# A two-layer decoder trunk with experts: weights of the experts loaded in 2 MB pieces, and the optional slots served after every piece

## The chip, the cores and the metric

The kernel runs on one core of one Trainium2 chip. The metric is device time in microseconds (us) of one execution; the figure compared is the median of several executions. One core has the engines PE (matrix products, with its weight loads, PEld), DVE and ACT (element-wise work out of PSUM and SBUF), POOL, and SP, which here issues the loads; 16 DMA engines move the data.

## The reference

256 tokens of width 1024 in float32 go through two layers. Layer 0 is retention (4 heads) and a dense SwiGLU of width 2816; layer 1 is a sparse attention with three branches and a mixture of experts. Each half is followed by a layer norm of alpha times its input plus its output. The part that the change touches is the mixture of experts:

```python
logits = (xf @ w_router).astype(jnp.float32)
top_v, top_i = lax.top_k(logits, TOP_K)              # 2 of 8 experts for each token
w = jax.nn.softmax(top_v, axis=-1)
gate = jnp.sum(jax.nn.one_hot(top_i, N_EXPERTS, dtype=jnp.float32) * w[..., None], axis=1)
for e in range(N_EXPERTS):
    out = out + gate[:, e:e + 1] * swiglu(xf, w_in[e], w_out[e])   # w_in 1024 x 7168, w_out 3584 x 1024
```

512 token places fall on 8 experts, 64 for each in the mean. The weights of one expert are 44 MB, of all eight 352 MB, and each is read once.

## The kernel before

All weights come from HBM through one ordered list of loads (`order`). A load (class `Raw`) is a tile of 128 partitions by 2048 floats: 1 MB, 8 KB in a row for each partition, laid out on the host so that it is contiguous. Units are the parts of a load that a step reads; when the last unit of a load has been read, `release` (L198) frees its buffer and at that point of the program issues the next load of the list. SP issues every load in program order. There are three kinds of buffers: 8 tiles `raw`, 2 tiles `more`, which come when the attention's buffers are given back (`moe_open`, L1316), and 6 tiles `ext`, which come when the buffers of split weights are given back (`moe_more`, L1323). So up to 16 MB of expert weights stand in SBUF. Ahead of the experts' list 87 single loads are made: 32 for the retention, 33 for the dense SwiGLU, 22 for the attention.

The work is a list of steps in a fixed order. An expert has 96 token places (slots) in three groups of 32, g = 0, 1, 2. Its hidden width is cut into four parts s = 0 to 3. For each part, `w_in` (L1192) multiplies the gathered tokens with 8 loads (4 for s = 3) of the input weights, `w_out` (L1250) multiplies the result of the part before with 4 loads (2 for s = 3) of the output weights, and then `h_transpose` (L1231) turns the hidden values. So an expert takes 28 + 14 = 42 loads, all experts 336. The step list puts `w_out` of a part behind `w_in` of the next one: `w_out` of the last part of expert e comes behind `w_in` of the first part of expert e + 1. The transposes for the scatter, the scatter itself and the gather for a later pair of experts stand between these steps.

Groups 0 and 1 are always computed, by `first` (L1206, L1264), load by load. Group 2 (slots 65 to 96) is needed only where more than 64 tokens chose the expert. Its count is in a register of PE; `rest` (L1214, L1274) holds a branch on it. It stands once in each `w_in` and each `w_out`, behind all loads of that step: where the count is over 64, PE reads all these loads again for group 2; where it isn't, `w_in` (and `w_out` of part 0) zeroes the PSUM bank of group 2 in the other arm. Both `first` and `rest` hold a unit of every load, so none of the loads of a step is released before its `rest`.

```python
            for i, u in enumerate(us):
                step([u[0]], first(i, u[0]), look=0)
            step([u[1] for u in us], rest, look=0)
```

The program is one instruction stream for each engine with semaphores between them.

Of the kernel before, what the change touches and what calls it, by code (L numbers as in the profile page):

```python
# [29 lines left out]
NE = 8  # L30
# [1 line left out]
NEG = -1e30  # L32

NRAW = 8
NMORE = 2
NEXT = 6
NHL = 6
LOOK = 3

# [36 lines left out]
class Raw:  # L76
    def __init__(self, parts):
        self.parts = parts
        self.kind = None
        self.last = False  # L80
        self.ap = None
        self.left = 0


class Unit:
# [10 lines left out]
def tile_decoder(ctx, tc, x, ret_w_in, ret_gn_g, ret_w_out, nsa_w_kv, cmp_k_pe, cmp_k_w1, cmp_k_w2,  # L96
# [76 lines left out]
    def raw(*parts):  # L173
        r = Raw(parts)
        raws.append(r)
        return r

    state = {"loaded": 0, "conv": 0, "raw": [], "more": [], "ext": []}

    def load(r):  # L180
        if r.kind == "more":
            r.ap = ptile([128, 2048], F32, "more", bufs=NMORE, lv=0)
        elif r.kind == "ext":
            r.ap = side["pool"].tile([128, 2048], F32, name="ext", tag="ext", bufs=NEXT)
        else:
            r.ap = sb.tile([128, 2048], F32, name="raw", tag="raw", bufs=NRAW)
        for view, src in r.parts:
            nc.sync.dma_start(view(r.ap), src)

    def load_next(kind="raw"):  # L190
        i = state["loaded"]
        if i < len(order) and not (kind != "raw" and order[i].last):
            state["loaded"] += 1
            order[i].kind = kind
            state[kind].append(order[i])
            load(order[i])

    def release(r):  # L198
        r.left -= 1
        held = state[r.kind]  # L200
        while held and held[0].left == 0:
            held.pop(0)
            load_next(r.kind)

    def convert(u, hi=None, lo=None):
        if not u.conv or u.hi is not None:
# [92 lines left out]
    def whole(n):  # L299
        return lambda a: a[:, :n]  # L300
# [75 lines left out]
    def ptile(shape, dt, tag, bufs=1, lv=-1):  # L376
        return phases[lv][1].tile(shape, dt, name=tag, tag=tag, bufs=bufs)
# [656 lines left out]
    if stop not in ("r1", "r2", "r3"):  # L1034
# [141 lines left out]
                                           skip_runtime_bounds_check_because="each of the S tokens counts at most once")  # L1176
            return f

        def units_m(block):

            r = raw((whole(2048), block))
            return [Unit(r, lambda a: a, conv=False) for _ in range(2)]

        def ws(s):
            return 256 if s < 3 else 128
# [6 lines left out]
        def w_in(e, s, us):  # L1192

            n, kl = 2 * ws(s), 8 // len(us)

            def mm(i, u, gs):
                v = u.view(u.raw.ap).rearrange("p (k j n) -> p k j n", k=kl, j=4)
                for g in gs:
                    for kk in range(kl):
                        k = i * kl + kk  # L1200
                        for j in range(4):
                            nc.tensor.matmul(M["A", g][j * 32:(j + 1) * 32, :n],  # L1202
                                             M["xg", e // 2][:, k, e % 2, g * 32:(g + 1) * 32], v[:, kk, j],
                                             start=k == 0, stop=k == KD - 1, skip_group_check=True)

            def first(i, u):  # L1206
                def f():
                    if i == 0:
                        for g in range(NG):
                            M["A", g] = bank("mm")  # L1210
                    mm(i, u, (0, 1))
                return f

            def rest():  # L1214
                with tc.If(M["n", e] > 64) as cmp:
                    for i, u in enumerate(us):
                        mm(i, u[1], (2,))
                with cmp.Else():
                    zero(M["A", 2])
                w = ws(s)  # L1220
                sh = ptile([128, NG, 256], F32, "msh")
                for g in range(NG):
                    nc.scalar.activation(sh[:, g, :w], M["A", g][:, :w], AF.Silu)  # L1223
                    nc.vector.tensor_mul(sh[:, g, :w], sh[:, g, :w], M["A", g][:, w:2 * w])  # L1224
                M["h"] = sh

            for i, u in enumerate(us):
                step([u[0]], first(i, u[0]), look=0)
            step([u[1] for u in us], rest, look=0)

        def h_transpose(s):  # L1231
            def f():
# [17 lines left out]
        def w_out(e, s, us):  # L1250

            hT = {}

            def mm(i, u, gs):
                v = u.view(u.raw.ap).rearrange("p (c h n) -> p c h n", c=2, h=2)
                for g in gs:
                    for c in range(2):
                        j, cc = (i, c) if s < 3 else (2 * i + c, 0)
                        for h in range(2):
                            q = (2 * h + c) * 32  # L1260
                            nc.tensor.matmul(M["y", g][q:q + 32], hT[0][:, g, cc, j * 32:(j + 1) * 32], v[:, c, h],  # L1261
                                             start=s == 0 and i == 0, stop=s == 3 and i == 1, skip_group_check=True)

            def first(i, u):  # L1264
                def f():
                    if i == 0:
                        hT[0] = M["hT"]
                        if s == 0:
                            for g in range(NG):
                                M["y", g] = bank("acc")  # L1270
                    mm(i, u, (0, 1))
                return f

            def rest():  # L1274
                with tc.If(M["n", e] > 64) as cmp:
                    for i, u in enumerate(us):
                        mm(i, u[1], (2,))
                if s == 0:
                    with cmp.Else():
                        zero(M["y", 2])  # L1280
                if s == 3:
                    y = ptile([128, 2, NG, 512], F32R, "yhl")
                    for g in range(NG):
                        if e < NE - 1:
                            split(y[:, 0, g], y[:, 1, g], M["y", g])
                        else:
                            nc.scalar.activation(y[:, 0, g], M["y", g], AF.Copy, scale=M["gs"][:, g:g + 1])  # L1287
                            nc.vector.scalar_tensor_tensor(y[:, 1, g], M["y", g], M["gs"][:, g:g + 1],  # L1288
                                                           y[:, 0, g].bitcast(F32), op0=ALU.mult, op1=ALU.subtract)
                    M["yhl"] = y  # L1290

            for i, u in enumerate(us):
                step([u[0]], first(i, u[0]), look=0)
            step([u[1] for u in us], rest, look=0)

        def scatter_mm(e, t, ps, start):

# [76 lines left out]
        for e in range(NE):  # L1374
            step([], count(e), look=0)
            for s in range(4):
                nl, nb = (8, 4) if s < 3 else (4, 2)
                w_in(e, s, [units_m(wst['moe_a'][28 * e + 8 * s + i]) for i in range(nl)])
                if prev:
                    w_out(*prev)  # L1380
                step([], h_transpose(s), look=0)
                if s == 0:
                    step([], transpose_S(e) if e == 0 else scatter(e - 1), look=0)
                    if e == 0:
                        step([], moe_gates, look=0)
                if s == 1 and e:
                    step([], transpose_S(e), look=0)
                if s == 2 and e % 2 and e < NE - 1:
                    step([], lambda j=e // 2 + 1: build_S(j), look=0)
                    for kq in range(4):  # L1390
                        step([], gather(e // 2 + 1, kq), look=0)
                if s == 2 and e == NE - 1:
                    step([], slot_gates, look=0)
                prev = e, s, [units_m(wst['moe_o'][14 * e + 4 * s + i]) for i in range(nb)]
        step([], sum_open, look=0)
        w_out(*prev)
        gbr = raw(*[(lambda a, i=i: a[:, i * D:(i + 1) * D],
# [82 lines left out]
    flat = [u for us, _, _ in steps for u in us]  # L1480
    order = []
    for u in flat:
        if u.raw not in order:
            order.append(u.raw)
    for _ in range(2):
        load_next()
    pos = 0
# [54 lines left out]
    yield w[:, 6].reshape(2, 2, 128, 1024).transpose(0, 2, 1, 3).reshape(2, 128, 2048)  # L1542


def _laid_out(v):
    ri, q, mi, mo = v['ret_w_in'][0], v['nsa_w_q'][0], v['moe_w_in'][0], v['moe_w_out'][0]
    return {
        'ret_b': _cols_b(ri[:, :2048]), 'ret_a': _cols_a(ri[:, 2048:]), 'ret_o': _rows(v['ret_w_out'][0]),
        'ffn_b': _cols_b(v['ffn_w_in'][0]), 'ffn_o': _rows(v['ffn_w_out'][0]),
        'kv_a': _cols_a(v['nsa_w_kv']), 'k_w1': _rows(v['cmp_k_w1']), 'v_w1': _rows(v['cmp_v_w1']),  # L1550
        'q0': _cols_a(np.concatenate([q[:, :256], q[:, 1024:]], 1), 304), 'q1': _cols_a(q[:, 256:1024], 256),
        'nsa_o': _rows(v['nsa_w_out'][0]),
        'moe_a': np.concatenate([b for e in range(NE) for b in _expert_in(mi[e])]),
        'moe_o': np.concatenate([b for e in range(NE) for b in _expert_out(mo[e])]),
    }


# [31 lines left out]
```

## Time and profile before

| | us |
|---|---|
| median of 3 runs | 1461.58 |
| runs | 1460.39 to 1463.45 |
| the profiled execution | 1460.46 |
| its span, first to last instruction | 1458.7 |
| PE busy | 1355.4 (93%) |
| PE weight loads busy | 755.2 (52%) |
| DVE busy | 471.3 (32%) |
| ACT busy | 347.0 (24%) |
| POOL busy | 62.7 (4%) |
| HBM read | 447.74 MB, 308 GB/s over the span |

The layers before the experts take about 588 us, the experts the rest. Busy time of PE is modelled to the end of each product, and products overlap; so the time of a load's products is taken from start to start. A product of float32 shows as two records: 16 records of `128x512` are the 8 products of one load for groups 0 and 1, 8 records are the 4 products of one load for group 2.

### The profile page before, as it was taken

Reading aid. Unit: us, or ns where it says so; the run is one execution under the profiler, and the core shown is the slowest. Engines: PE = TensorE matmul, PEld = TensorE weight load, DVE = VectorE, ACT = ScalarE, POOL = GpSimd, SP = SyncE. Lnnn points to the kernel's source line nnn. Section 1 sums busy time; section 2 is a strip of 40 time slices with the busy share of each in tenths; the row PEclk is TensorE's granted clock in tenths of the full one; section 3 lists DMA queues with packets and bytes.
Section 4 is the critical chain, followed back from the end, with each engine's and each line's share of the span. In section 5 each row is a group of like instructions: output and inputs, shape, how many; then the busy total and the mean of one; then the engine's idle time right before and its main releaser. Section 6 shows DMA issues by size and latency. Waiting matters only on the chain. (4 is left out here: it accounts for less than half of the span.)

```text
span 1458.7 us, 25366 instructions
## 1 busy us (share of the span) xinstructions
PE 1355.4 (93%) x11073; PEld 755.2 (52%) x11073; DVE 471.3 (32%) x845; ACT 347.0 (24%) x653; POOL 62.7 (4%) x74
## 2 busy tenths in 40 slices
PE   8999999999999988998999988888999988889995
PEld 7888888999978657432334332232333342222341
DVE  5755875554674886100100201001101101001002
ACT  4433434434534562200101110011001010000002
POOL 3101101000011000100000000000000000000000
PEclk9999999999999898999999999999999999999997
DMA  9736444544615308599999999999999999999970
GB/s 388 271 139 220 158 168 176 201 180 173 250 59 209 124 1 319 209 418 419 419 419 418 412 418 419 419 418 419 419 416 416 419 419 419 419 418 419 418 306 32
DMA packets 64022, 450.78 MB, mean 309 GB/s; under 512 B 7233, under 2 KB 7393, under 8 KB 10641
## 3 DMA queue, kind: packets, MB, share of 16 engines
q1 hardware_dynamic: 62208, 443.77, 75.4%
q0 software_dynamic: 1536, 4.98, 1.0%
q8 instruction: 106, 1.74, 0.5%
q14 instruction: 28, 0.22, 0.0%
q10 hardware_dynamic: 144, 0.07, 0.0%
HBM read 447.74 MB, written 1.05 MB: 308 GB/s over the span
## 5 line engine op out<-in xcount | busy, mean ns | idle before, releaser
L1202 PE MATMUL mm<-raw,xg 128*32 128x512 f32 (+1 forms) x2416 | 242.9, 544 | 11.5 <-DMA raw<-w_moe_a_dram 11.4
L1224 DVE TENSOR_TENSOR msh<-msh,mm 128x256 f32<-128x256 f32 (+1 forms) x96 | 35.5, 387 | 509.3 <-ACT msh L1223 509.3
L215 DVE TENSOR_TENSOR wlo<-raw,whi 128x1024 fp32r<-128x1024 f32 (+2 forms) x162 | 187.6, 1208 | 32.1 <-ACT whi L214 31.8
L1202 PE MATMUL mm<-ext,xg 128*32 128x512 f32 (+1 forms) x1808 | 178.8, 538 | 14.5 <-DMA ext<-w_moe_a_dram 14.5
L1202 PEld LDWEIGHTS mm<-raw,xg 128*32 128x32 f32 x2416 | 74.5, 110 | 164.4 <-issue 119.1
L214 ACT CAST whi<-raw 128x1024 fp32r<-128x1024 f32 (+2 forms) x162 | 153.7, 1008 | 18.6 <-PE acc L224 12.2
L1223 ACT ACTIVATE msh<-mm 128x256 f32<-128x256 f32 (+1 forms) x96 | 32.4, 357 | 492.9 <-PE mm L1202 492.9
L348 PE MATMUL mm<-xTh,whi 128*128 128x256 f32 x448 | 126.5, 282 | 1.6 <-ACT whi L214 1.6
L350 PE MATMUL mm<-xTh,wlo 128*128 128x256 f32 x448 | 125.9, 281 | 0.5 <-DVE wlo L215 0.5
L1261 PE MATMUL acc<-raw,hT 128*32 128x512 f32 x1000 | 116.5, 594 | 10.4 <-DMA raw<-w_moe_o_dram 9.2
L349 PE MATMUL mm<-xTl,whi 128*128 128x256 f32 x448 | 125.7, 281 | 0.0
L1202 PEld LDWEIGHTS mm<-ext,xg 128*32 128x32 f32 x1808 | 55.2, 110 | 129.3 <-issue 77.8
L1261 PE MATMUL acc<-ext,hT 128*32 128x512 f32 x864 | 98.4, 594 | 8.7 <-DMA ext<-w_moe_o_dram 8.7
L348 PEld LDWEIGHTS mm<-xTh,whi 128*128 128x128 f32 x448 | 84.7, 189 | 3.1 <-ACT whi L214 2.0
L350 PEld LDWEIGHTS mm<-xTh,wlo 128*128 128x128 f32 x448 | 84.7, 189 | 0.8 <-DVE wlo L215 0.8
L349 PEld LDWEIGHTS mm<-xTl,whi 128*128 128x128 f32 x448 | 84.7, 189 | 0.8
L1246 DVE COPY hT<-mm 128x256 f32<-128x256 f32 (+1 forms) x32 | 12.4, 389 | 223.2 <-PE mm L1239 223.2
L1261 PEld LDWEIGHTS acc<-raw,hT 128*32 128x32 f32 x1000 | 31.9, 110 | 87.9 <-issue 61.5
L1244 ACT COPY hT<-acc 128x512 f32<-128x512 f32 (+1 forms) x32 | 17.1, 536 | 230.6 <-PE acc L1239 150.1
L1202 PE MATMUL mm<-more,xg 128*32 128x512 f32 (+1 forms) x640 | 65.1, 535 | 4.9 <-DMA more<-w_moe_a_dram 4.8
L1261 PEld LDWEIGHTS acc<-ext,hT 128*32 128x32 f32 x864 | 26.4, 110 | 76.1 <-issue 50.8
L222 PE MATMUL mm<-whi,xTh 128*128 128x512 f32 (+1 forms) x144 | 55.6, 386 | 0.2 <-ACT xTh L227 0.2
(325 smaller groups left out, 1676.4 us busy)
## 6 DMA issues: line engine op xcount, KB each, us to landing
raw<-w_moe_a_dram SPq DMA_DIRECT2D x113, 1024.0 KB, 19.9
ext<-w_moe_a_dram SPq DMA_DIRECT2D x82, 1024.0 KB, 19.9
raw<-w_moe_o_dram SPq DMA_DIRECT2D x55, 1024.0 KB, 19.9
ext<-w_moe_o_dram SPq DMA_DIRECT2D x44, 1024.0 KB, 19.9
more<-w_moe_a_dram SPq DMA_DIRECT2D x29, 1024.0 KB, 19.9
raw<-w_ffn_b_dram SPq DMA_DIRECT2D x22, 1024.0 KB, 5.0
raw<-w_ret_a_dram SPq DMA_DIRECT2D x16, 1024.0 KB, 8.9
more<-w_moe_o_dram SPq DMA_DIRECT2D x13, 1024.0 KB, 19.9
```

Of the source, the lines that this page charges most:

```text
L214: nc.scalar.copy(u.hi, v)
L215: nc.vector.tensor_sub(u.lo, v, u.hi.bitcast(F32))
L222: nc.tensor.matmul(ps, xh, wh, start=start, stop=False, skip_group_check=True)
L348: nc.tensor.matmul(ps, u.hi[:, k], xh[:, k], start=start and k == 0, stop=False, skip_group_check=True)
L349: nc.tensor.matmul(ps, u.hi[:, k], xl[:, k], start=False, stop=False, skip_group_check=True)
L350: nc.tensor.matmul(ps, u.lo[:, k], xh[:, k], start=False, stop=k == KD - 1, skip_group_check=True)
L1202: nc.tensor.matmul(M["A", g][j * 32:(j + 1) * 32, :n], M["xg", e // 2][:, k, e % 2, g * 32:(g + 1) * 32], v[:, kk, j], start=k == 0, stop= ...
L1223: nc.scalar.activation(sh[:, g, :w], M["A", g][:, :w], AF.Silu)
L1224: nc.vector.tensor_mul(sh[:, g, :w], sh[:, g, :w], M["A", g][:, w:2 * w])
L1244: nc.scalar.copy(dst, src)
L1246: nc.vector.tensor_copy(dst, src)
L1261: nc.tensor.matmul(M["y", g][q:q + 32], hT[0][:, g, cc, j * 32:(j + 1) * 32], v[:, c, h], start=s == 0 and i == 0, stop=s == 3 and i == 1, ...
```

## The change

Two neighbouring loads of one expert step become one of 2 MB (class `Slot`, with `wide` as its source). The host lays the two blocks out side by side (`_pairs`), so that each partition has 16 KB in a row. The 8 `raw` tiles become one tile `ring` of 8 places; a single load takes one place, a pair two neighbouring ones, and a pair that would begin at an odd place leaves one place empty until that pair is released. `more` is one tile of 2 MB, `ext` are three. A pair is released when both of its halves have been read. `rest` is called behind every second load, for these two alone; the zeroing arm and the element-wise work stay with the last call (the zeroing of `w_out` with its first).

```diff
-NMORE = 2
-NEXT = 6
+NMORE = 1
+NEXT = 3
...
+    ring = sb.tile([128, NRAW * 2048], F32, name="ring")
+    state = {"at": 0, "free": NRAW, "loaded": 0, "conv": 0, "raw": [], "more": [], "ext": []}
+
+    def load(z):
+        n = len(z.raws)
+        if z.kind == "more":
+            ap = ptile([128, n * 2048], F32, "more", bufs=NMORE, lv=0)
+        elif z.kind == "ext":
+            ap = side["pool"].tile([128, n * 2048], F32, name="ext", tag="ext", bufs=NEXT)
         else:
-            r.ap = sb.tile([128, 2048], F32, name="raw", tag="raw", bufs=NRAW)
-        for view, src in r.parts:
-            nc.sync.dma_start(view(r.ap), src)
+            i = (state["at"] + z.room - n) % NRAW
+            state["at"] += z.room
+            ap = ring[:, i * 2048:(i + n) * 2048]
+        if z.wide is not None:
+            nc.sync.dma_start(ap, z.wide() if callable(z.wide) else z.wide)
...
+            if kind == "raw":
+                n = len(order[i].raws)
+                order[i].room = n + state["at"] % n
+                if state["free"] < order[i].room:
+                    return False
+                state["free"] -= order[i].room
...
     def release(r):
         r.left -= 1
-        held = state[r.kind]
-        while held and held[0].left == 0:
-            held.pop(0)
-            load_next(r.kind)
+        kind = r.slot.kind
+        held = state[kind]
+        while held and all(q.left == 0 for q in held[0].raws):
+            z = held.pop(0)
+            if kind != "raw":
+                load_next(kind)
+            else:
+                state["free"] += z.room
+                while load_next():
+                    pass
...
-            def rest():
+            def rest(i):
                 with tc.If(M["n", e] > 64) as cmp:
-                    for i, u in enumerate(us):
-                        mm(i, u[1], (2,))
+                    for j in (i, i + 1):
+                        mm(j, us[j][1], (2,))
+                if i + 2 < len(us):
+                    return
                 with cmp.Else():
                     zero(M["A", 2])
...
             for i, u in enumerate(us):
                 step([u[0]], first(i, u[0]), look=0)
-            step([u[1] for u in us], rest, look=0)
+                if i % 2:
+                    step([v[1] for v in us[i - 1:i + 1]], lambda i=i: rest(i - 1), look=0)
...
+def _pairs(blocks):
+
+    b = np.concatenate(list(blocks))
+    return b.reshape(-1, 2, 128, 2048).transpose(0, 2, 1, 3).reshape(-1, 128, 4096)
```

## Rows read from the trace of the kernel before

**Rows 1.** The page's 40 slices: busy tenths of DMA, then GB/s.
```profile
DMA  9736444544615308599999999999999999999970
GB/s 388 271 139 220 158 168 176 201 180 173 250 59 209 124 1 319 209 418 419 419 419 418 412 418 419 419 418 419 419 416 416 419 419 419 419 418 419 418 306 32
```
**Rows 2.** Busy time by stretch: PE, PEld, DVE, ACT, POOL; PEclk, DMA share, GB/s.
```profile
590.00:600.00 10.00, 10.00 (x96) 2.99 (x92) 0.00 (x0) 0.33 (x1) 0.00 (x0) 1.00 0.01 2
...
646.00:1310.00 664.00, 606.58 (x5871) 211.72 (x5871) 68.66 (x155) 59.40 (x143) 5.94 (x12) 1.00 1.01 418
740.00:840.00 100.00, 98.25 (x1000) 37.73 (x993) 11.80 (x27) 9.88 (x23) 1.02 (x2) 1.00 1.01 416
...
1326.00:1438.00 112.00, 111.23 (x1093) 40.53 (x1087) 12.58 (x26) 10.37 (x24) 0.00 (x0) 1.00 0.79 323
```
**Rows 3.** Timeline of PE, head of expert 7: start, us, operation, count [idle <-releaser].
```profile
1305.27 1.92 PE L1261 MATMUL acc<-raw,hT 128*32 128x512 f32 x16 [0.58 <-DMA raw<-w_moe_o_dram]
1307.37 0.41 PE L1239 MATMUL acc<-ident,msh 128*128 128x128 f32 x2 [0.18 <-PEq L1275]
...
1307.97 1.92 PE L1202 MATMUL mm<-raw,xg 128*32 128x512 f32 x16
1310.24 1.93 PE L1202 MATMUL mm<-raw,xg 128*32 128x512 f32 x16 [0.35 <-DMA raw<-w_moe_a_dram]
...
1325.19 1.92 PE L1202 MATMUL mm<-ext,xg 128*32 128x512 f32 x16 [0.57 <-DMA ext<-w_moe_a_dram]
1326.93 2.76 PE L1202 MATMUL mm<-raw,xg 128*32 128x512 f32 x24
...
1332.08 1.90 PE L1202 MATMUL mm<-ext,xg 128*32 128x512 f32 x16
1333.80 3.62 PE L1261 MATMUL acc<-ext,hT 128*32 128x512 f32 x32
```
**Rows 4.** Timeline of SP: the loads issued from 468 to 607 us.
```profile
468.89 84.29 SPq L188 DMA_DIRECT2D raw<-w_moe_a_dram  x7
553.29 0.85 SPq L188 DMA_DIRECT2D more<-w_moe_a_dram  x2
560.45 0.33 SPq L188 DMA_DIRECT2D raw<-w_moe_a_dram  x1
569.23 3.50 SPq L188 DMA_DIRECT2D ext<-w_moe_a_dram  x6
602.61 1.97 SPq L188 DMA_DIRECT2D raw<-w_moe_o_dram  x4
```
**Rows 5.** Timeline of PE, head of expert 0.
```profile
588.45 12.22 PE L1202 MATMUL mm<-raw,xg 128*32 128x512 f32 x112
600.49 1.90 PE L1202 MATMUL mm<-more,xg 128*32 128x512 f32 x16
602.20 0.40 PE L1189 MATMUL mm<-zb 128*32 128x512 bf16 x4
```
**Rows 6.** DMA from 646 to 1310 us: packets, MB; then the loads' own queue.
```profile
DMA packets 38040, 277.53 MB, mean 418 GB/s; under 512 B 4223, under 2 KB 4223, under 8 KB 4223
...
q1 hardware_dynamic: 37976, 276.52, 100.6%
```
**Rows 7.** DMA from 700 to 1300 us by queue: packets, MB, share of 16 engines.
```profile
q1 hardware_dynamic: 34309, 249.82, 100.6%
q8 instruction: 54, 0.88, 0.6%
```
**Rows 8.** DMA from 450.5 to 455 us, mostly rows of 4 KB.
```profile
DMA packets 448, 1.80 MB, mean 400 GB/s; under 512 B 49, under 2 KB 49, under 8 KB 408
...
q1 hardware_dynamic: 448, 1.80, 99.0%
```
**Rows 9.** Branches of `w_in` (L1215) and `w_out` (L1275): ns min/median/max.
```profile
L1215 PEldq COMPARE_BRANCH  x44: 65/179/860, 599.6 to 1416.8; - x44
L1275 PEldq COMPARE_BRANCH  x44: 65/178/357, 623.0 to 1435.0; - x44
```

More of the change, by code (lines that the diff above doesn't have):

```diff
@@ L78, in __init__ @@
         self.parts = parts
-        self.kind = None
+        self.slot = None
         self.last = False
@@ L82, in __init__ @@
         self.left = 0
+class Slot:
+    def __init__(self, raws, wide=None):
+        self.raws = raws
+        self.wide = wide
+        self.last = raws[0].last
+        self.kind = None
+        self.room = 0
+        for r in raws:
+            r.slot = self
 class Unit:
@@ L176, in raw @@
         return r
[L178 to L184, printed above, removed]
-        else:
-            r.ap = sb.tile([128, 2048], F32, name="raw", tag="raw", bufs=NRAW)
-        for view, src in r.parts:
-            nc.sync.dma_start(view(r.ap), src)
+    ring = sb.tile([128, NRAW * 2048], F32, name="ring")
[6 more added lines that the diff above has]
+            ap = side["pool"].tile([128, n * 2048], F32, name="ext", tag="ext", bufs=NEXT)
+        else:
+            i = (state["at"] + z.room - n) % NRAW
[3 more added lines that the diff above has]
+            nc.sync.dma_start(ap, z.wide() if callable(z.wide) else z.wide)
+        for i, r in enumerate(z.raws):
+            r.ap = ap[:, i * 2048:(i + 1) * 2048]
+            for view, src in r.parts:
+                nc.sync.dma_start(view(r.ap), src)
     def load_next(kind="raw"):
@@ L196, in load_next @@
             load(order[i])
+            return kind == "raw"
     def release(r):
         r.left -= 1
-        held = state[r.kind]
-        while held and held[0].left == 0:
-            held.pop(0)
-            load_next(r.kind)
+        kind = r.slot.kind
[8 more added lines that the diff above has]
+                    pass
     def convert(u, hi=None, lo=None):
@@ L1177, in count, with units_m @@
             return f
-        def units_m(block):
-            r = raw((whole(2048), block))
-            return [Unit(r, lambda a: a, conv=False) for _ in range(2)]
+        def units_m(w, e, i, n):
+            us = []
+            for j in range(0, n, 2):
+                rs = [raw() for _ in range(2)]
+                Slot(rs, w[e, (i + j) // 2])
+                us.extend([Unit(r, lambda a: a, conv=False) for _ in range(2)] for r in rs)
+            return us
         def ws(s):
@@ L1272, in first, with rest @@
                 return f
-            def rest():
+            def rest(i):
                 with tc.If(M["n", e] > 64) as cmp:
-                    for i, u in enumerate(us):
-                        mm(i, u[1], (2,))
-                if s == 0:
+                    for j in (i, i + 1):
+                        mm(j, us[j][1], (2,))
+                if s == 0 and i == 0:
                     with cmp.Else():
@@ L1293, in w_out @@
                 step([u[0]], first(i, u[0]), look=0)
-            step([u[1] for u in us], rest, look=0)
+                if i % 2:
+                    step([v[1] for v in us[i - 1:i + 1]], lambda i=i: rest(i - 1), look=0)
         def scatter_mm(e, t, ps, start):
@@ L1377, in tile_decoder @@
                 nl, nb = (8, 4) if s < 3 else (4, 2)
-                w_in(e, s, [units_m(wst['moe_a'][28 * e + 8 * s + i]) for i in range(nl)])
+                w_in(e, s, units_m(wst['moe_a'], e, 8 * s, nl))
                 if prev:
@@ L1393, in tile_decoder @@
                     step([], slot_gates, look=0)
-                prev = e, s, [units_m(wst['moe_o'][14 * e + 4 * s + i]) for i in range(nb)]
+                prev = e, s, units_m(wst['moe_o'], e, 4 * s, nb)
         step([], sum_open, look=0)
@@ L1482, in tile_decoder @@
     for u in flat:
-        if u.raw not in order:
-            order.append(u.raw)
+        if u.raw.slot is None:
+            Slot([u.raw])
+        if u.raw.slot not in order:
+            order.append(u.raw.slot)
     for _ in range(2):
@@ L1552, in _laid_out @@
         'nsa_o': _rows(v['nsa_w_out'][0]),
-        'moe_a': np.concatenate([b for e in range(NE) for b in _expert_in(mi[e])]),
-        'moe_o': np.concatenate([b for e in range(NE) for b in _expert_out(mo[e])]),
+        'moe_a': np.stack([_pairs(_expert_in(mi[e])) for e in range(NE)]),
+        'moe_o': np.stack([_pairs(_expert_out(mo[e])) for e in range(NE)]),
     }
```

## The prediction

> **What bounds the kernel now.** I read the 40 slices first. From about 620 us to 1390 us the DMA engines are full, at 412 to 419 GB/s; before that they are not, and one slice shows 1 GB/s [rows 1]. The reader is to see two regimes: up to the experts the order of the work on PE sets the time, and in the experts the stream of weights does. Next I asked for the stages. Between 646 and 1310 us the DMA share is 1.01, while PE's modelled busy time leaves 57 us open [rows 2]. The last stretch, 1326 to 1438 us, is the other way round: PE is busy for 111.2 of 112 us, DMA for 0.79 [rows 2]. The timeline of PE shows where it turns. In part 0 of expert 7 PE waits before each load but the first, the loads coming 2.5 us apart; at 1326.93 it begins the group-2 products of all eight loads, and from there it does not wait for a load again [rows 3]. So the end is: arrival of the first loads of expert 7, then PE's own work.
>
> Two costs stand on this path that the slices hide. First, the engines move 2 GB/s between 590 and 600 us [rows 2]. SP's timeline says why: 16 loads (7 + 2 + 1 + 6) are issued by 573 us and the next one only at 602.61 [rows 4], behind the zeroing at 602.20 that ends the first `rest` [rows 5]. All 16 buffers were full, and none of the first eight was given back until PE had read all eight. Second, PE has open time while it waits for the eight loads at 1307 to 1325, and then spends 1333.80 - 1326.93 = 6.87 us on group 2 of the same loads [rows 3].
>
> **The change part by part.**
>
> *First release.* A load costs PE (600.49 - 588.45) / 7 = 1.72 us for groups 0 and 1 [rows 5]. The first pair is read at 588.45 + 3.44 = 591.9; with a branch and the issue I put the next issue at 592.1, 10.5 us before the 602.61 of now. But there is less in SBUF then. The 87 single loads leave the ring at an odd place, so the first pair takes three places; with the four loads of the attention's output weights ahead of it only three pairs fit until then. With one `more` and three `ext` that is 7 pairs, 14 MB, in place of 16. Release of the first pair frees four places and starts two pairs at once. The stream begins 10.5 us earlier and 2 loads behind. In 664 us 4223 / 16 = 264 loads come in, 2.515 us each [rows 6], so 5.0 us of the gain go back: **-5.5 us**. Bounds: -10.5 if all 16 MB stood there, and +5.0 if the release came no earlier. I take the middle one, as both terms are counted from the code's order. The stream should not break behind it: PE releases a pair each 3.4 us, and a pair takes 5 us to come.
>
> *Rows of 16 KB.* How much of the engines' time goes to the packet rather than to bytes? In 4.5 us with mostly 4 KB rows, 16 x 4.5 x 0.990 = 71.3 us of engine time moved 1.80 MB in 448 packets: 39.60 us and 249 packets a MB [rows 8]. In the saturated stage 16 x 600 x 1.006 = 9658 us moved 249.82 MB in 34309 packets: 38.66 us and 137.3 packets a MB [rows 7]. The difference is 0.94 us for 111.6 packets, 8.4 ns a packet. A 2 MB load has 8 rows and one completion packet on each engine, 144 for 2.097 MB, 68.7 a MB: 68.6 fewer, 0.58 us of 38.66, 1.49%. From the issue at 602.61 (+2 us) to load 294 at 1310.24 there are 278 loads in 705.6 us [rows 3, 4]; 1.49% is **-10.5 us**. Bounds: 0 if the engines cut 16 KB rows again, -21 if the whole packet cost went (137.3 x 8.4 ns is 3.0%).
> Here a rule of the Trainium skill gives another size. DMA: Bandwidth & Descriptors, Why small descriptors are slow (HBM only), puts the fixed cost of a packet at about 3 cycles of a 32-byte path and finds joining them worthwhile only up to 256 B. By it an 8 KB row costs 259 cycles, two of them 518 in place of 515, 0.6%, an estimate of 4 us, and the sum would be 1449. The rows show 8.4 ns, more than that, and I keep them.
>
> *Head of expert 7.* The last load of the first pair is load 294: 7 x 42, less the two `w_out` loads of expert 6 that come behind part 0, plus two. It was there at 1310.24, and its part 0 ended at 1333.80, 23.6 us later [rows 3]. With the branch behind each pair PE needs 3 groups x 2 loads x 0.86 = 5.17 us a pair, and pairs come each 5.0; so it works through without a wait, 4 x 5.17 = 20.7 us: **-2.9 us**, at best; 0 if the four branches take 0.7 us each. PE is ready for that pair: behind load 292 it has 3.4 us of products and 0.9 of transposes, less than the 5.0 to the next pair. Behind that, everything is the same PE work, and the last loads are early: at 1333.80 PE falls further behind, not nearer.
>
> *Branches.* `rest` goes from 8 to 21 calls an expert, 64 to 168 in all. The 44 compares of `w_in` are 32 entries and 12 jumps out of the three experts over 64 (1, 4 and 7), so a taken branch is two of them, of 179 ns in the middle [rows 9]. On PE they stand beside products already issued: from 1325.19 to the first of group 2 it is 1.74 us, from 1332.08 to the products behind the jump 1.72, as in any dense stretch [rows 3]; that cover is PE's backlog. Where it is empty, 0.18 us shows at 1307.37 [rows 3]. While PE waits for the stream, this has 1.5 us a pair to hide in. Only expert 7 pays: 13 more branches, at 0 to 0.18 each, 0 to 2.3 us; I take **+0.4**, near the dense rows.
>
> *Nothing.* In experts 1 and 4 PE is slower than the stream (126 x 0.86 = 108 us of products against 105), and lies back; the stream keeps 416 GB/s there [rows 2] because 16 buffers cover it, and pairs are given back sooner than eights. The layers before keep single loads with the same waits; 0. The 2 MB grain would cost at the end, but the end is PE's.
>
> Sum on the profiled execution: 1460.46 - 5.5 - 10.5 - 2.9 + 0.4 = 1442.0. It lies 1.1 below the median of the runs, so for a median I say **1442.5**.
>
> **The rivals.**
> *The rows are cut.* The change asks for 16 KB rows, but nothing of this queue here shows one; if packets stay at 8 KB, the -10.5 falls to about nothing: 1453. For it: no row of that size; against: the instruction queue moves 0.88 MB in 54 packets, 16 KB each [rows 7].
> *More than counted.* The ring holds 16 MB at the start, or the packet cost falls by more: 5 to 10 us more, 1433 to 1437.
> *Branches decide (slower).* In expert 7 there is no cover if PE's backlog runs out at each branch. The longest compare was 0.86 us [rows 9]; two of these for each of 13 branches are 22.4 us, which makes 1464. It decides from 18.9 / 13 = 1.45 us a branch on. Against it: no idle beside the taken ones in rows 3.
> *Long rows are slow (slower).* The 54 instruction packets took 0.006 x 9600 / 54 = 1.07 us each [rows 7], against 0.28 us for the mean packet of the loads. If a 16 KB row went at that pace, a pair would take 8.6 us, and 139 pairs some 490 us more: 1930. With the other terms at -8.0 it decides as soon as a pair takes 5.08 + 8.0 / 139 = 5.13 us, 1% over two loads now. Against it: those are fetches into another place. [...]
> *Nothing seen.* Cut rows and branches of half a microsecond or more eat one another's gain: 1458 to 1464.
>
> **How the numbers follow.** Forecast 0.55 (1436 to 1449), cut rows 0.17, more than counted 0.10, branches 0.08, slow rows 0.04, nothing seen 0.06. The range 1433 to 1456 takes the first two and most of the third, 0.78. A measurement of this kernel tells about 0.2%, 3 us, from no change. Faster is forecast, cut rows and more: 0.82; the same 0.06; slower 0.12.
>
> **What would show it.** SP's first issue behind the 14 MB at about 592, two pairs at once; the slice at 590 to 600 us no longer empty; 424 to 425 GB/s in the saturated stage and half the packets; expert 7 beginning near 1292 us and its part 0 taking 21 us without a wait; no idle behind the branches there. Wrong would be: 418 GB/s again; SP waiting for a zeroing or the end of a step; gaps in PE of some tenths at each branch of expert 7; or the layers before the experts moving by more than 1 us.

## The result and the profile after

The changed kernel takes 1443.74 us (median of 4 runs, 1442.2 to 1446.61) against 1462.16 (4 runs, 1460.39 to 1463.45): ratio 0.9871, 95% interval 0.9847 to 0.9895. The profiled execution took 1444.41 us with a span of 1442.5, which is 16.2 less than before.

The GB/s of the page's slices, and the loads' queue (packets, MB, share of 16 engines' span):
```profile
GB/s 386 270 137 228 152 186 145 198 203 192 176 152 149 144 1 214 330 426 424 426 426 425 426 425 424 426 424 426 426 426 426 426 425 426 425 425 426 425 269 33
...
q1 hardware_dynamic: 38016, 443.76, 75.1%
```
Where [rows 1] has 412 to 419 in the saturated slices, this has 424 to 426. Busy time by stretch (PE, PEld, DVE, ACT, POOL, then granted clock, DMA share, GB/s), and then the loads' queue from 700 to 1250:
```profile
575.00:597.00 22.00, 18.58 (x93) 13.50 (x93) 6.45 (x22) 6.25 (x9) 6.40 (x3) 0.55 0.72 308
590.00:600.00 10.00, 9.66 (x67) 4.03 (x70) 0.00 (x0) 2.00 (x3) 0.42 (x1) 0.76 0.33 97
646.00:1290.00 644.00, 604.74 (x5904) 230.43 (x5896) 69.44 (x157) 59.88 (x145) 5.92 (x12) 0.99 1.01 425
1300.00:1420.00 120.00, 119.23 (x1171) 44.47 (x1167) 11.60 (x25) 9.91 (x23) 0.00 (x0) 1.00 0.78 331
```
```profile
q1 hardware_dynamic: 16010, 233.18, 100.0%
```
There are 68.7 packets a MB where [rows 7] has 137.3, so the 16 KB rows were not cut, and the queue's rate is 424.0 GB/s over 550 us against 416.4 there. The hole at 590 us is smaller than in [rows 2] but not gone. At the end PE is the bound as before, busy for 119.2 of 120 us.

SP's loads (start, us until the last issue, count), to be read against [rows 4]:
```profile
474.89 78.50 SPq L204 DMA_DIRECT2D ring<-w_moe_a_dram  x3
553.49 0.38 SPq L204 DMA_DIRECT2D more<-w_moe_a_dram  x1
569.42 1.28 SPq L204 DMA_DIRECT2D ext<-w_moe_a_dram  x3
570.74 0.59 SPq L204 DMA_DIRECT2D ring<-w_moe_a_dram  x1
596.86 4.44 SPq L204 DMA_DIRECT2D ring<-w_moe_o_dram  x2
```
PE at the second half of the router and at the head of expert 0, then at the head of expert 7 (start, busy us, count, idle and releaser), to be read against [rows 3, 5]:
```profile
577.32 3.58 PE L1080 MATMUL mm<-rt_w,yhl 128*128 128x8 f32 x16
...
591.36 5.34 PE L1239 MATMUL mm<-ring,xg 128*32 128x512 f32 x32
597.03 3.80 PE L1239 MATMUL mm<-ring,xg 128*32 128x512 f32 x32 [0.34 <-PEq L1252]
...
1284.82 3.64 PE L1301 MATMUL acc<-ring,hT 128*32 128x512 f32 x32 [1.52 <-DMA ring<-w_moe_o_dram]
1290.58 5.34 PE L1301 MATMUL acc<-ring,hT 128*32 128x512 f32 x32 [2.12 <-DMA ring<-w_moe_o_dram]
1296.65 5.36 PE L1239 MATMUL mm<-ring,xg 128*32 128x512 f32 x48
1301.79 5.36 PE L1239 MATMUL mm<-more,xg 128*32 128x512 f32 x48
1306.94 10.51 PE L1239 MATMUL mm<-ext,xg 128*32 128x512 f32 x96
1317.24 3.64 PE L1301 MATMUL acc<-ext,hT 128*32 128x512 f32 x32
```
The same half of the router in the kernel before:
```profile
575.52 3.58 PE L1047 MATMUL mm<-rt_w,yhl 128*128 128x8 f32 x16
```
The reader is to see three things in the changed kernel. The first pair of expert 0 takes 5.34 us and ends at 596.7, and only then does SP issue. Part 0 of expert 7 goes through without a wait. And the pair ahead of it, at 1290.58, is as slow as the first one of expert 0.

From these rows the 16.2 us can be cut at points of the path:

| stretch | before | after | difference |
|---|---|---|---|
| first load issued behind the 16 MB | 602.61 | 596.86 | -5.75 |
| from there to the first pair of expert 7 in SBUF | 707.6 | 698.0 | -9.6 |
| PE late for that pair | 0 | 1.8 | +1.8 |
| part 0 of expert 7 | 23.56 | 20.59 | -2.97 |
| from its end to the end of the span | 124.9 | 125.2 | +0.3 |

The 698.0 of the changed kernel is read from runs 7, 8 and 10 below, where PE waits for that pair (697.8 to 698.0). In this profile PE came to it later: by these runs the pair was due at 596.86 + 698.0 = 1294.9, and PE began at 1296.65. Each row of the table is from single profiles.

### The profile page after: what moved, and what is told of

It is laid out like the page before. It is cut to its first block, busy times and chain, and to the rows that moved or that the text cites. A ratio compares the mean times of both kernels' runs of the same rounds, so it can differ in the third digit from the quotient of the medians.

```text
span 1442.5 us, 25322 instructions
## 1 busy us (share of the span) xinstructions
PE 1354.2 (94%) x11073; PEld 777.8 (54%) x11073; DVE 471.3 (33%) x845; ACT 346.8 (24%) x653; POOL 62.7 (4%) x74
## 5 line engine op out<-in xcount | busy, mean ns | idle before, releaser
L1239 PE MATMUL mm<-ring,xg 128*32 128x512 f32 (+1 forms) x2336 | 235.8, 554 | 9.9 <-DMA ring<-w_moe_a_dram 5.9
L248 DVE TENSOR_TENSOR wlo<-ring,whi 128x1024 fp32r<-128x1024 f32 (+2 forms) x162 | 187.7, 1208 | 32.4 <-ACT whi L247 32.1
L1239 PE MATMUL mm<-ext,xg 128*32 128x512 f32 (+1 forms) x1888 | 182.8, 536 | 6.0 <-DMA ext<-w_moe_a_dram 3.0
L1239 PEld LDWEIGHTS mm<-ring,xg 128*32 128x32 f32 x2336 | 77.7, 111 | 157.9 <-issue 133.6
L247 ACT CAST whi<-ring 128x1024 fp32r<-128x1024 f32 (+2 forms) x162 | 153.7, 1008 | 18.9 <-PE acc L257 12.2
L1239 PEld LDWEIGHTS mm<-ext,xg 128*32 128x32 f32 x1888 | 66.3, 111 | 114.7 <-issue 93.9
L1301 PE MATMUL acc<-ring,hT 128*32 128x512 f32 x1040 | 119.2, 600 | 7.5 <-DMA ring<-w_moe_o_dram 6.5
L1301 PE MATMUL acc<-ext,hT 128*32 128x512 f32 x848 | 94.9, 593 | 4.5 <-DMA ext<-w_moe_o_dram 4.2
L1301 PEld LDWEIGHTS acc<-ring,hT 128*32 128x32 f32 x1040 | 36.8, 111 | 82.2 <-issue 70.1
L1284 ACT COPY hT<-acc 128x512 f32<-128x512 f32 (+1 forms) x32 | 17.1, 535 | 223.1 <-PE acc L1279 146.9
```

What stands on the lines that cost most here:

```text
L247: nc.scalar.copy(u.hi, v)
L248: nc.vector.tensor_sub(u.lo, v, u.hi.bitcast(F32))
L1239: nc.tensor.matmul(M["A", g][j * 32:(j + 1) * 32, :n], M["xg", e // 2][:, k, e % 2, g * 32:(g + 1) * 32], v[:, kk, j], start=k == 0, stop= ...
L1284: nc.scalar.copy(dst, src)
```

## The experiments

**1. The branch alone.** The kernel before, its 1 MB loads kept, with the branch behind every second load:
```
-            step([u[1] for u in us], rest, look=0)
+                if i % 2:
+                    step([v[1] for v in us[i - 1:i + 1]], lambda i=i: rest(i - 1), look=0)
```


> Only the second half of the change: loads stay 1 MB with 8 KB rows in 16 tiles, and rest stands behind every second load. Theory (three separate terms: earlier first release, longer rows, no burst at the head of expert 7): the stream stays at 418 GB/s and 2.515 us a load, SP's first issue behind the 16 loads comes at about 592 us in place of 602.6 (-10.5), part 0 of expert 7 takes 21 us behind its second load (-2.9), 13 branches there cost 0.4; about 1449 us. Rival (all of the gain is the longer rows): 1460 to 1462.


1449.78 us, ratio 0.9911 (0.9883 to 0.9939). SP's first issue, and PE's first load of expert 7's first complete pair and the end of part 0:
```profile
592.89 4.82 SPq L188 DMA_DIRECT2D raw<-w_moe_o_dram  x4
```
```profile
1302.71 5.36 PE L1202 MATMUL mm<-raw,xg 128*32 128x512 f32 x48 [0.40 <-DMA raw<-w_moe_a_dram]
...
1321.86 3.62 PE L1264 MATMUL acc<-ext,hT 128*32 128x512 f32 x32
```
Of the gain of 12.7 us in the span (1446.0), 7.5 lie before expert 7 (1310.24 to 1302.71), 4.4 in part 0 (19.15 us), 0.8 behind it. The rate over 700 to 1250 us stays at 416.8 GB/s. The theory that the rows give everything falls. Two readings need care. SP's first issue is 9.7 us earlier than before, but expert 7 only 7.5: the stretch between them takes 709.8 us against 707.6, so the finer branch alone makes it 2.2 us longer. And the 19.15 us begin behind the products of the pair's first load, as 23.56 before does, while the changed kernel's 20.59 hold both loads of the pair, 1.72 us more.

**2. The loads alone.** The changed kernel with the branch once a step again:
```
-                if i % 2:
-                    step([v[1] for v in us[i - 1:i + 1]], lambda i=i: rest(i - 1), look=0)
+            step([u[1] for u in us], rest, look=0)
```


> Only the first half of the change: 2 MB loads with 16 KB rows, rest once a step as before. Theory: 425 GB/s and 2.477 us a load, 9 to 12 us less by load 294; SP's first issue behind 16 MB stays behind the zeroing of part 0, at 603 to 606 us (expert 0 may start up to 3 us later, as in the changed kernel); the burst at the head of expert 7 stays. About 1452 us. Rival (rest for each pair gives all): 1460 to 1464.


1461.3 us, ratio 0.9974 (0.9954 to 0.9994): a smaller gain than I expected. The window in expert 1, SP's first issue, and PE in expert 7:
```profile
740.00:840.00 100.00, 98.44 (x1001) 37.79 (x1005) 11.65 (x27) 10.42 (x25) 1.02 (x2) 1.00 0.98 410
```
```profile
607.11 0.80 SPq L204 DMA_DIRECT2D ring<-w_moe_o_dram  x2
```
```profile
1306.35 3.64 PE L1239 MATMUL mm<-ring,xg 128*32 128x512 f32 x32 [0.66 <-DMA ring<-w_moe_a_dram]
...
1331.28 3.62 PE L1298 MATMUL acc<-ext,hT 128*32 128x512 f32 x32
```
The stream takes 699.2 us from first issue to this pair, 8.4 less than before, but it starts 4.5 us later than before, and part 0 takes 24.9 us. From 740 to 840 us, mostly in expert 1, whose branch is taken, the DMA share is 0.98 and the rate 410 GB/s, against 1.01 and 425 in the changed kernel; SP waits up to 17.5 us there for PE to give a pair back, in the changed kernel up to 10.9. That pairs held for a whole step come free too late is the likely reason. Still, the two halves of the change very nearly add up: the profiled spans fall by 12.7 us with the branch alone, 2.7 with the loads alone and 16.2 with both, and the ratios 0.9911 and 0.9974 multiply to 0.9885 against 0.9871. So these runs don't show that the wide loads need the finer branch. They gain 8.4 us in the stream and lose 4.5 ahead of it; with the finer branch they lose 4.0 there (596.86 against run 1's 592.89).

**3. Row or load?** The change, each 2 MB load made of two rows of 8 KB a partition, apart in HBM:
```
-            nc.sync.dma_start(ap, z.wide() if callable(z.wide) else z.wide)
+            nc.sync.dma_start(ap.rearrange("p (b n) -> p b n", b=2), z.wide.rearrange("b p n -> p b n"))
```


> The changed kernel with the two 1 MB blocks of a pair left apart in HBM: loads of 2 MB, two rows of 8 KB for each partition. Theory (the row length sets the rate): 130 packets a MB, 418 to 419 GB/s, 9 to 12 us lost against the changed kernel in the stream; up to 3 us given back because the layer norm's rows on the POOL queue land as early as before; 1450 to 1455. Rival (the size of a load, or the number of completions, sets the rate): 425 GB/s and 1443.


1452.06 us, ratio 0.9913 (0.989 to 0.9935). The loads' queue from 700 to 1250 us:
```profile
q1 hardware_dynamic: 29761, 229.49, 100.6%
```
417.3 GB/s and 129.7 packets a MB, against 424.0 and 68.7: the rate follows the row, not the load. With the engines taken as full, a MB costs 16 x 550 / 229.49 = 38.35 us of engine time, against 16 x 550 / 233.18 = 37.74: 0.61 us for 61 packets, an estimate of 10 ns each. With the shares 1.006 and 1.000, as the prediction reckoned, it would be 14.

**4 and 5. Long rows in 1 MB loads.** Each pair by two loads, of partitions 0 to 63 and 64 to 127 (4), or of the even and the odd ones (5):
```
+            for h in (0, 64):
+                nc.sync.dma_start(ap[h:h + 64], z.wide[h:h + 64])
```
```
+            w = z.wide.rearrange("(q h) n -> h q n", h=2)
+            for h in range(2):
+                nc.sync.dma_start(ap.rearrange("(q h) n -> h q n", h=2)[h], w[h])
```


> The changed kernel with each pair brought by two loads of 64 partitions, 1 MB each with 16 KB rows. Theory (the row length sets the rate): 425 GB/s or a tenth of a per cent under it for the second completion packet, 1443 to 1446. Rival (the size of a load sets the rate): 418 GB/s and 1452 to 1455.

> The changed kernel with each pair brought by two loads of 1 MB and 16 KB rows, one of the even partitions and one of the odd ones. The run with partitions 0 to 63 and 64 to 127 apart moved only 214 GB/s, so it did not answer what it was for. Theory (the row length sets the rate; there it was the half of the partitions that all loads in flight wrote into): 424 to 426 GB/s, 1443 to 1447. Rival (loads of 1 MB or of 64 partitions are slow with long rows): 214 to 418 GB/s, 1452 and up.


Run 4: 2164.58 to 2225.93 us, ratio 1.486; run 5: 1446.44 us, ratio 0.9895 (0.988 to 0.991). The loads' queue from 700 to 1250 us, of 4 and then of 5:
```profile
q1 hardware_dynamic: 8941, 117.23, 100.6%
```
```profile
q1 hardware_dynamic: 17734, 232.44, 100.0%
```
Run 4 missed its purpose: it changed which partitions a load writes as well, and at 213 GB/s that covers everything else. Run 5 has its row length, load size and number of loads and goes at 422.6 GB/s. So the loss of 4 is due to the block of 64 neighbouring partitions, or to the order in which it takes the rows of the source, which changes with it. Run 5 answers the question: with 16 KB rows even 1 MB loads run at nearly the rate of the change.

**6. The `more` load later.** Expert 0 starts 2.9 us later than before, and the trace shows two causes. DVE waits for the rows of the last layer norm, after and then before:
```profile
567.58 1.28 DVE L314 SCALAR_TENSOR_TENSOR msh<-msh,mv,ygb 128x1024 f32<-128x1024 f32 x1 [1.63 <-DMA ygb<-in_ln_g_dram]
```
```profile
565.79 1.28 DVE L281 SCALAR_TENSOR_TENSOR msh<-msh,mv,ygb 128x1024 f32<-128x1024 f32 x1
```
These rows (0.5 MB, POOL's queue) land 10.4 us after their issue, before 7.1; just ahead of them SP has asked for 4 MB of pairs in place of 3 MB of single loads. And the granted clock is 0.55 over 575 to 597 us, where the kernel before has 0.72. The clock is low in both, for 20.5 us here and 13.7 before. The rows divide the 2.9 us: the second half of the router starts 1.8 us later (577.32 against 575.52), behind DVE's wait, and 1.1 more are lost from there to expert 0. This run takes away the wait: the `more` load is issued in the next step, behind those rows.


> The changed kernel with the one load into more issued behind the attention, with the ext loads (569 us in place of 553 us), so that only one pair is under way when POOL asks for the layer norm's rows. Theory (expert 0 starts 3 us later than before because these rows land at 567.5, 3.3 us later, behind 4 MB of pairs; DVE waits 1.6 us): the wait of DVE falls to 0 to 0.4 us, expert 0 starts 1.5 to 3 us earlier, the end comes as much earlier, 1441 to 1443. Rival (the later start is the low clock alone): no move, 1443 to 1445. If the 16 MB are then not there when they are needed, 1445 to 1448.


1445.49 us, ratio 0.9876 (0.9857 to 0.9895). DVE's wait is gone, but the profiled run was 7 us late already from the attention, where the clock fell to 0.5 three times (at about 463, 491 and 511 us). By time it is inconclusive. The trace says more: from the router's first product to expert 0 it takes 18.65 us, where the change takes 20.18 and the kernel before 18.14. Of the 1.5 us less, 1.4 lie between the two halves of the router, where PE waits 1.5 us for DVE's rows and in the change 2.9.

**7. The clock alone.** 17 products of zeros in PE's gaps between the router and expert 0 (the zeros are now set by POOL and no longer by DVE):
```
+        def warm(n):
+            for _ in range(n):
+                nc.tensor.matmul(M["dum"], zb[:, 0:128], zb, start=True, stop=True, skip_group_check=True)
...
+            warm(9)     # behind router(0); warm(4) twice more at the rank products
```


> The changed kernel with 17 products of zeros (128x512, bf16) in PE's gaps between the router and the gather of expert 0. Theory (the granted clock lies at 0.5 from 576 to 596 us, which stretches the router, the gather and the first pair, and so the first release): the clock stays at 1.0 or comes back earlier there, SP's first issue falls from 597 to 590 to 593, the end comes 3 to 6 us earlier: 1438 to 1441. Rival (the chain on DVE sets the start whatever the clock): at most 1.7 us from the first pair, 1442 to 1444.


1438.18 us (1437.77 to 1445.77), ratio 0.9851 (0.983 to 0.9872). The stretch ahead of expert 0; PE's first pair and the first pair of expert 7; SP's first issue:
```profile
575.00:597.00 22.00, 18.88 (x142) 11.27 (x145) 6.24 (x21) 6.26 (x9) 6.40 (x3) 0.92 0.89 362
```
```profile
588.48 3.64 PE L1247 MATMUL mm<-ring,xg 128*32 128x512 f32 x32
...
1290.16 5.36 PE L1247 MATMUL mm<-ring,xg 128*32 128x512 f32 x48 [0.66 <-DMA ring<-w_moe_a_dram]
```
```profile
592.27 4.29 SPq L204 DMA_DIRECT2D ring<-w_moe_o_dram  x2
```
With the clock at 0.92, expert 0 starts 2.9 us earlier, its first pair takes 3.64 us in place of 5.34, and the next load is issued 4.6 us earlier. DVE's wait for the norm's rows is still there (1.83 us). Expert 7 begins 6.5 us earlier. One of the five runs, 1445.77 us, has a mean granted clock of 0.982, as the slower runs of the change have; the others have 0.990 or 0.991. So the products don't hold the clock in every run.

**8. Both, and the second fall of the clock.** Edits 6 and 7, and five zero products between the two pairs of the last `w_out` part ahead of expert 7:
```
+                if (e, s, i) == (NE - 2, 2, 1):
+                    step([], warm_late, look=0)
```


> Both of these, and 5 such products between the two pairs of expert 6's third w_out, where PE waits 2.1 us and the granted clock falls just ahead of expert 7. Theory: the gains add, 1.6 + 4 + 1, 1435 to 1439. Rival (the stream comes no earlier, as 16 MB have to be in first): 1440 to 1444.


1436.65 us (1435.21 to 1437.23), ratio 0.9824 (0.981 to 0.9837): faster than both kernels. The same rows as of run 7:
```profile
575.00:597.00 22.00, 20.34 (x159) 11.09 (x161) 6.58 (x21) 6.17 (x9) 6.38 (x3) 0.92 1.01 423
```
```profile
1289.10 5.36 PE L1247 MATMUL mm<-ring,xg 128*32 128x512 f32 x48 [0.66 <-DMA ring<-w_moe_a_dram]
```
```profile
591.09 4.29 SPq L204 DMA_DIRECT2D ring<-w_moe_o_dram  x2
```
The stream now never stops between 575 and 597 us (423 GB/s). Against the change, the issue is 5.8 us earlier and PE's 1.8 us at expert 7 are gone, 7.6 of the 7.8 us between the spans (1434.7 and 1442.5).

**9. Twice as many branches.** The change with a branch behind each load, 336 in all:
```
             def rest(i):
+                with tc.If(M["n", e] > 64):
+                    mm(i, us[i][1], (2,))
                 with tc.If(M["n", e] > 64) as cmp:
-                    for j in (i, i + 1):
-                        mm(j, us[j][1], (2,))
+                    mm(i + 1, us[i + 1][1], (2,))
```


> The changed kernel with the branch of rest once for each load (two for each pair): 336 in place of 168 in all, 42 in place of 21 in expert 7; the products are the same. Theory (a branch that is taken hides behind products already issued; one that is not taken shows 0.2 to 0.35 us, and only expert 0 has no wait of the stream to hide it): part 0 of expert 7 stays at 20.6 to 21 us, the end moves by 0 to 2 us against the changed kernel's 125.2 us behind part 0 and 1443.7 in all. Rival (branches decide): 0.3 us or more for each of 21 further branches in expert 7, 6 us and up, 1450 or later.


1469.3 us, ratio 1.0043 (1.0027 to 1.0059): my expectation failed. What PE waited for from 588 to 1297 us (us, count, longest; PEq is PE's sequencer, where its branches stand), of the change and then of this run, and this run's part 0 of expert 7:
```profile
PE mm L1239 <- PEq L1252: 7.8, 41, 0.5
PE acc L1301 <- DMA ring<-w_moe_o_dram: 6.5, 5, 2.1
PE mm L1239 <- DMA ring<-w_moe_a_dram: 5.9, 5, 2.2
PE acc L1301 <- DMA ext<-w_moe_o_dram: 4.2, 4, 1.3
...
PE acc L1279 <- PEq L1315: 3.3, 19, 0.2
```
```profile
PE mm L1239 <- PEq L1254: 30.3, 49, 0.9
PE acc L1280 <- PEq L1321: 10.6, 17, 0.8
PE acc L1302 <- PEq L1321: 6.2, 14, 0.6
PE mm L1226 <- PEq L1252: 5.8, 12, 0.6
```
```profile
1316.53 5.36 PE L1239 MATMUL mm<-ring,xg 128*32 128x512 f32 x48
...
1337.13 3.64 PE L1302 MATMUL acc<-ext,hT 128*32 128x512 f32 x32
```
The rival's time came, but not at its place. Expert 7, whose branches are taken, has the same part 0 as the change (20.6 us). The loss stands in the experts whose branches are not taken: over 697 to 803 and 1013 to 1118 us, in experts 1 and 4, PE idles 0.6 us each at branches, and in the stretches of the other experts 10.3 to 11.3 each. In all it idles 52.9 us at branches, where the change has 12.1 (7.8 + 3.3 + 1.0 in a row not shown), and no longer waits for the stream, for which the change waits 22.1 us (the three rows above and two of 3.0 and 2.5 that are left out). The 40.8 us more, less 22.1, are 18.7; expert 7 begins 19.9 us later.

**10. The change once more.** No edit.


> The changed kernel itself, beside the run before it. All theories: 1442 to 1447. If the spread comes from the granted clock, as the theory has it, a profile with less time at half clock between 490 and 600 us shows an earlier first issue and an earlier end by the same amount; 698 us lie between the first issue behind the 16 MB and the first pair of expert 7 in either.


1440.84 us, ratio 0.9868 (0.9851 to 0.9884). Its rows at the two places where the clock fell in the first profile:
```profile
575.00:597.00 22.00, 18.66 (x113) 13.98 (x117) 6.36 (x22) 6.26 (x9) 6.40 (x3) 0.63 0.78 319
```
```profile
1287.84 3.64 PE L1301 MATMUL acc<-ring,hT 128*32 128x512 f32 x32 [1.33 <-DMA ring<-w_moe_o_dram]
...
1292.83 5.36 PE L1239 MATMUL mm<-ring,xg 128*32 128x512 f32 x48 [0.65 <-DMA ring<-w_moe_a_dram]
...
1308.91 5.36 PE L1239 MATMUL mm<-ext,xg 128*32 128x512 f32 x48 [0.43 <-DMA ext<-w_moe_a_dram]
1314.09 3.62 PE L1301 MATMUL acc<-ext,hT 128*32 128x512 f32 x32
```
SP's first issue:
```profile
595.03 4.29 SPq L204 DMA_DIRECT2D ring<-w_moe_o_dram  x2
```
Here the wait ahead of the last `w_out` pair is 1.33 us and not 2.12, the clock stays up, and that pair takes 3.64 us. So the +1.8 belongs to a run, not to the kernel; the low clock ahead of expert 0 is there both times (17.1 us of it here, 20.5 in the first profile). It ends here before the first pair, which takes 3.64 us, and SP's first issue comes 1.8 us earlier than in the first profile, expert 7 3.8 us earlier. Part 0 takes 21.26 us, with a wait of 0.43 us for the last pair.

## Why the prediction was right, and where by luck

The forecast was 1442.5 us, from -5.5, -10.5, -2.9 and +0.4.

**First release: the sum was right, both terms were wrong.** I counted 14 MB in SBUF and an issue at 592.1. In fact all 16 MB stood there, 3 + 1 + 3 + 1 pairs: the fourth ring pair is issued at 570.74 us. In the order of the program that load stands behind the first release, and I took this for a wait; but SP waits only for the places that the load overwrites, and those (the skipped place and that of the last attention load) were free by then. So the 5.0 us that I gave back for 2 loads were not lost. The issue, though, came at 596.86 and not at 592.1, since expert 0 began 2.9 us later and its first pair ran at the low clock. The two errors, 5.0 and 4.8, cancel. Runs 7 and 8 show what was covered: with the clock at 0.92 the issue comes at 592.27 and 591.09, and run 8's 1436.65 us is what the rival "more than counted" priced for 16 MB at the start (1433 to 1437). The term that I left out is that the pairs change the stages ahead of the experts, which I put at 0: expert 0 starts 2.9 us later, more than the 1 us that I had named as a sign of being wrong.

**Rows: right, though -9.6 is not the rows alone.** The stretch holds 2.2 us that the finer branch adds (run 1, 709.8 us). Against run 1 the long rows save 11.8 us, without the finer branch 8.4 (run 2); the forecast of 10.5 lies between. The 8.4 ns a packet from [rows 7, 8] become 10 in run 3, by a rougher reckoning, and run 3 against the change leaves no other cause for the rate than the row (417.3 to 424.0 GB/s, 1.6%). The Trainium skill (DMA: Bandwidth & Descriptors, Why small descriptors are slow (HBM only)), by which I put the gain at 0.6% as an estimate, is too low here; the measurement decides.

**Head of expert 7: right.** -2.97 against -2.9, in 20.59 us without a wait, as 4 x 5.17 said. PE came 1.8 us late to that pair, which helped; where it came in time, part 0 took 20.6 us (runs 7 and 8) and 21.3 (run 10). Run 2, without the finer branch, has 24.9 there, and run 1, without the long rows, 19.2, or 20.9 with the first load's 1.72: the branch is the cause.

**Branches: small, as forecast, but wrong in reason.** +0.3 against +0.4 behind the head can't be told from nothing: there runs 7, 8 and 10 have 125.4, 125.0 and 124.8 us, the kernel before 124.9. The taken ones are hidden, as [rows 3] let one expect. Wrong is that the others have "1.5 us a pair to hide in". PE does wait for the stream, 22.1 us until expert 7, where the kernel before waits 45.7. But in the change these waits stand only between 908 and 1013 us and from 1118 us on: from the head of expert 0 to expert 3, and in expert 4, PE lies behind the stream and has no such slack. The branches not taken eat 12.1 us, 22.1 are left, and twice as many branches use them up (run 9). So the rival of run 9, 0.3 us or more for each further branch, had the right price and the wrong expert: 40.8 us over the 105 further branches of the five experts that don't take them is about 0.4 us each.

**Not foreseen: the clock.** +1.8 ahead of expert 7 in the profiled run, and a part of the late first release. Of the 4.8 us by which the first pair ends later than counted (596.7 against 591.9), about 1.8 lie with the norm's rows and 2.8 with the low clock (1.1 up to expert 0, 1.7 in the first pair); in run 10, whose first pair runs at the full clock, the issue comes at 595.03. Over the nine runs of the changed kernel the time follows the mean granted clock: 0.980 to 0.982 with 1444.35 to 1446.61 us, 0.984 to 0.986 with 1440.17 to 1443.07. That zero products move the issue by 4.6 us (run 7) shows what a higher clock gives back there. It doesn't show that the change lowered the clock: the kernel before has it low ahead of expert 0, too, for 13.7 us. What makes the clock fall in one run at 1291 us and not in another is shown only as far as the wait ahead of it. The pair ran slow behind waits of 2.12, 2.08 (run 5) and 2.44 us (run 3), and at full speed behind 1.33 (run 10), 1.47 (run 6) and 1.85 us (run 7).

## What to carry to other kernels

Where the trace has two row lengths, a price per packet can be worked out from them and moved to a third. Try the halves of a change apart: here the finer branch alone gave 0.9%, the wide loads alone 0.3% and both 1.3%, so most of the gain came from giving buffers back earlier, and the wide loads lost part of theirs in a stage ahead of the one that they were meant for. A wait that costs an engine "nothing" because it has slack must be set against all that the slack is used for, above all where another stage lives on it.

## What the runs showed of the hardware

- The 64 neighbouring partitions of run 4 ran at 213 GB/s, the even or odd ones of run 5 at 422.6, with the same row and load. The order of the source's rows changes with the partitions. That the rows then under way all go to one half of the partitions is argued, not shown.
- How late 0.5 MB on another queue lands depends on what is under way: 7.1 us from issue to landing behind 3 MB with 8 KB rows (before, run 1), 8.9 behind 4 MB with 8 KB rows (run 3), 10.4 behind 4 MB with 16 KB rows (the change), and 10.2 where these come in 1 MB loads (run 5). With the same bytes and rows the size of a load changes 0.2 us.
- Where branches are not taken, PE idles at 66 places in the change, 0.18 us in the mean and 0.5 at most; with two branches for each pair, at 92 places, 0.58 us in the mean and 0.9 at most (run 9). A taken one shows none in expert 7, where PE has work queued.
- The granted clock fell to 0.5, which is 1.2 GHz, behind a PE wait of 2.12 us, for 3.4 us. Zero products in the gaps ahead of expert 0 held it at 0.92 there in the profiles of runs 7 and 8.
